# Layer 0's attention issued from a written table, and the second attention's first work drawn into the latent input's last rounds

## The chip, the cores and the metric

The kernel runs on one core of one Trainium2 chip. A core has TensorE (PE: matrix products into PSUM), VectorE (DVE), ScalarE (ACT) and GpSimd (POOL) for elementwise work, and SyncE (SP), which issues most transfers. Each engine works through its own queue in order and waits on semaphores for the others. The metric is the device time in microseconds, from the first to the last instruction with a little around it; lower is better. The program is launched once and computes two whole transformer layers.

## The reference, cut to what matters

```python
for i in range(2):
    h = rms_norm(x, attn_norm_g[i])
    x = x + (diff_attention(h, ...) if i == 0 else mla_attention(h, ...))
    h = rms_norm(x, ffn_norm_g[i])
    x = x + conv_ffn(h, ffn_w_up[i], ffn_conv_w[i], ffn_conv_b[i], ffn_w_down[i])
return rms_norm(x, final_norm_g)

def diff_attention(h, ...):            # 1024 tokens, 8 heads, each with two 64-wide parts c
    q, k, v = jnp.split(h @ w_qkv, 3, axis=-1)
    q, k = rotary on the first 16 of each 64, v is 128 wide
    lam = jnp.exp(jnp.sum(lq1 * lk1)) - jnp.exp(jnp.sum(lq2 * lk2)) + lambda_init
    def block(qb, blk):                # 128 queries at a time, keys up to their 64-token chunk
        p = masked_softmax(jnp.einsum('bqhcd,bkhcd->bhcqk', qb, k) * 64 ** -0.5, mask)
        return jnp.einsum('bhqk,bkhe->bqhe', p[:, :, 0] - lam * p[:, :, 1], v)
    return (rms_norm(o, subln_g) * (1.0 - lambda_init)).reshape(b, s, D_MODEL) @ w_o

def mla_attention(h, ...):             # 16 heads, from latents of rank 384 (q) and 256 (kv)
    proj = h @ w_in
    c_q, c_kv = rms_norm(proj[..., :384]), rms_norm(proj[..., 384:640])
    k_pe = apply_rope(proj[..., 640:])
    q = c_q @ w_uq; k_nope, v = c_kv @ w_ukv
    softmax((q_nope k_nope + q_pe k_pe) * 96 ** -0.5) @ v, then @ w_o
```

All of it is float32; the kernel gets near that with products of split operands.

## The kernel before

**Products.** Every float32 operand is split into a high part (a cast, `hi`, on ScalarE, L127) and a low part (the difference, `lo`, on VectorE or GpSimd, L130), and `mm3` makes one product of three matmuls (L119 to L121). Tiles in SBUF lie in named places of three sizes, `s`, `u` and `h`; PSUM holds two score tiles of two banks (`S`), three single banks (`b`) and one bank `u`, in which the projections gather. These letters are the tile names in the profile.

**Layer 0's attention** (`diff_attention`, `steps`, `DaStep`). The work is 32 steps, t = 4h + p: head h, quarter p, which takes the 256 queries of the row tiles 2p and 2p + 1 (j = 0, 1). A step computes scores for both parts c (L1622, L1623; the j-th row of quarter p has (2p + j + 1) x 128 keys), their maximum on VectorE (L1627, L1631), the exponential on ScalarE (L1637), the reciprocal of the sums (L1647), the product of one with -lambda (L1648), the scaling of part 0 (L147 or L149), and the mix of both parts on VectorE (L1650). One step later the mixed probabilities are transposed (L252), split, and multiplied with v; the quarters 1 and 3 end with a norm over 512 queries (`finish`), one step later still. `rsqrt` in it takes Identity, Ln, Exp and Square on ScalarE (L174 to L177) and two operations on VectorE.

Between these lie the projections of q, k and v, half a sequence at a time: units of 24 matmuls in bank `u` (`da_unit`). `da_complete` frees the bank by a copy on ScalarE for v (L556) or by a shuffle and a product on VectorE for q and k (L237, L238), and goes on with the rotary part (GpSimd, L239 and L240) and the splits. A unit gives its PSUM bank up to the next one only when that is done.

**Order.** `steps` writes the pieces in a plain sequence: scores 0, half a unit, transposes of the step before, weigh 0, scores 1, the rest of the units, the product of the step before, weigh 1, the norm. That sequence is only a priority: a scheduler then sets the order on each engine. Some parts of the kernel are marked `manual_schedule`, and there the engines named take the order as written; the attention steps are not among them.

**The seam to the second attention** (`mla_input`, `mla_heads`). Eight rounds compute the latents of one row tile each (S), followed by transposes into `cq` and `ckv`, and two rounds behind, `values` computes v, copies it to a buffer (ScalarE, L1407) and stores it to `v_d`. The buffers of these copies and of the fetched weights (`self.raw`) are two places used in turn, u14 and u15. In round 7 `heads.first()` projects the first keys and queries; the 64 steps of the second attention are written after round 9, through the same `steps`.

Of the kernel before, what the change touches and what calls it, by code (L numbers as in the profile page):

```python
# [13 lines left out]
ALU = mybir.AluOpType  # L14
# [42 lines left out]
class Trunk:  # L57
# [155 lines left out]
    def load_constants(self):  # L213
# [6 lines left out]
        nc.vector.tensor_scalar_mul(self.g_sub, self.g_sub, 1.0 - LAMBDA_INIT)  # L220
# [60 lines left out]
    def steps(self, attend, units, prepare, n):  # L281
# [3 lines left out]
        for t in range(n + 2):  # L285
# [10 lines left out]
            self.run(u, 1)  # L296
            if before:
                before.turn()
            if now:
                now.weigh(0)  # L300
                now.scores(1)
# [5 lines left out]
            if t >= 2:  # L307
                steps[t - 2].finish()


    def diff_attention(self, o_d, prefetch):
# [24 lines left out]
        def split_w(h, which):  # L336
            if h < DA_HEADS:
                raw = raws.pop((h, which))
                w = self.w([P, 2, D], F32R)
                self.hi(w[:, 0, :], raw)  # L340
                self.lo(w[:, 1, :], raw, w[:, 0, :], nc.gpsimd)
                heads[h]["w", which] = w[:, 0, :], w[:, 1, :]

        def unit(h, which, half):
            hd = heads[h]
            return self.da_unit(R, H, hd["w", which], which, half, hd, tab)
# [168 lines left out]
        def prepare(t):  # L515
            h, p = divmod(t, 4)
            if p == 0:
                split_w(h + 1, 1)
                fetch_w(h + 1, 0)
            if p == 1:  # L520
                split_w(h + 1, 0)
                fetch_w(h + 1, 2)
            if p == 2:
                split_w(h + 1, 2)
            if p == 3:
                fetch_w(h + 2, 1)
            if h + 1 == DA_HEADS:
                prefetch()

# [7 lines left out]
        self.steps(lambda t: DaStep(self, R, *divmod(t, 4), heads, o_d), units, prepare, 4 * DA_HEADS)  # L537

    def da_unit(self, R, H, W, which, half, hd, tab):
# [9 lines left out]
        yield from self.da_complete(R, acc, which, half, hd, tab)  # L549

# [783 lines left out]
    def mla_input(self, W, hts, turns, v_d, heads_of):  # L1334
# [89 lines left out]
        for i in range(NT + 2):  # L1424
            if readies:
                readies.pop(0)()
            if i == NT - 1:
                heads.share(1, 0)
                heads.first()
# [19 lines left out]
            if i == NT:  # L1449
                rotary(1)  # L1450
                heads.share(1, 1)
        return heads

    def mla_heads(self, cT, v_d, o_d):
# [5 lines left out]
        v_ring, q_ring, t_ring = self.ring("s13", "s4"), self.ring("s1", "s10", "s5", "s9"), self.ring("h10", "h11", "h8")  # L1460
        k_places, kT = ["s0", "s11", "s12", "s8"], []
# [3 lines left out]
            P=self.ring("u6", "u7", "u8", "u9", "u12"), pT=self.ring("u0", "u1", "u10", "u11"), o=self.ring("h4", "h5", "h6", "h7"),  # L1465
# [59 lines left out]
        def first():  # L1525
# [496 lines left out]
```

## Time and profile before

| | |
|---|---|
| median of 3 runs | 2427.79 us (2427.32 to 2431.45) |
| the profiled execution | 2430.68 us, its span 2428.9 us |
| TensorE busy | 2355.0 us (97%) |
| VectorE, ScalarE, GpSimd busy | 1916.0, 1305.3, 618.5 us |
| granted TensorE clock, mean | 0.996 |
| layer 0's attention, heads 0 to 6 | 53 to 459 us of the span |
| the seam between latent input and second attention | 1329 to 1366 us |

Matmuls overlap and their ends are modelled, so a busy TensorE is not one that starts a matmul as often as it could. A row of the waits gives who waited for whom, the time in total, how often, and the longest. A row of a timeline gives start, duration, engine, line, operation, tiles written and read, and in brackets the idle time before it and what ended it.

### The profile page before, as it was taken

To read this page: it belongs to the slowest core of one execution; us is meant where nothing else is said; L and a number is where in the kernel's file an instruction comes from. 1 tells how busy PE (TensorE), PEld (TensorE's weight loads), DVE (VectorE), ACT (ScalarE), POOL (GpSimd) and SP (SyncE) were. 2 spreads that over 40 slices of the span, in tenths; PEclk is the share of its full clock that TensorE was granted. 3 is DMA by queue.
4 is the path that set the end of the run, shared out by engine and by line. 5 is a ranking of instruction groups with operands and counts; after the bars stand their busy time and mean duration, and the time that the engine had idled before them with its cause. 6 is when DMAs were issued, how large, how long until landed. Compare 5 with 4: busy or idle time off the path is not lost.

```text
span 2428.9 us, 32660 instructions
## 1 busy us (share of the span) xinstructions
PE 2355.0 (97%) x11936; PEld 1997.5 (82%) x11936; DVE 1916.0 (79%) x3111; ACT 1305.3 (54%) x2446; POOL 618.5 (25%) x489
## 2 busy tenths in 40 slices
PE   7999999999999999999999999999999999999998
PEld 6888787887888888878899788988878888887886
DVE  6667776857888888889964777887488888888997
ACT  5677777755444444444445777776244444444444
POOL 4545454424100000000041666665330000000001
PEclk9999999999999999999999999999999999999999
DMA  4111111223322222554221211114322222227502
GB/s 161 40 35 44 35 35 44 100 93 100 99 82 79 87 78 88 187 175 131 72 103 46 77 40 29 49 59 134 96 87 87 79 87 87 78 86 278 172 3 78
DMA packets 95792, 213.91 MB, mean 88 GB/s; under 512 B 8720, under 2 KB 33936, under 8 KB 95632
## 3 DMA queue, kind: packets, MB, share of 16 engines
q1 hardware_dynamic: 86448, 184.04, 23.1%
q10 hardware_dynamic: 9184, 27.79, 3.1%
q8 instruction: 94, 1.54, 0.3%
q14 instruction: 66, 0.54, 0.1%
HBM read 159.37 MB, written 52.43 MB: 87 GB/s over the span
## 4 chain that ended last, share of the span: by engine, by line
PE 82%; DVE 7%; ACT 5%; DMA 3%; issue 2%; POOL 1%; SPq 0%; DVEq 0%; POOLq 0%; ACTq 0%
PE S L119 13%; PE S L121 13%; PE S L120 13%; PE b L119 8%; PE b L120 8%; PE b L121 8%; PE u L119 4%; PE u L120 4%; PE u L121 4%; PE b L252 3%; DMA u<-g_d 2%; PE u L1727 1%; DVE s L130 1%; PE u L1726 1%; ACT s L127 1%
## 5 line engine op out<-in xcount | busy, mean ns | idle before, releaser
L167 POOL TENSOR_TENSOR st<-st,mhalf 128x1 f32<-128x1 f32 x56 | 36.6, 654 | 1314.1 <-DVE st L164 1305.5
L127 ACT CAST u<-h 128x512 fp32r<-128x512 f32 (+2 forms) x242 | 145.9, 619 | 297.4 <-DVE h L847 277.7
L119 PE MATMUL S<-s,u 128*128 128x512 f32 (+1 forms) x768 | 290.5, 378 | 7.6 <-ACT s L127 2.6
L121 PE MATMUL S<-s,u 128*128 128x512 f32 (+1 forms) x768 | 289.5, 377 | 0.1
L120 PE MATMUL S<-s,u 128*128 128x512 f32 (+1 forms) x768 | 289.4, 377 | 0.0
L119 PE MATMUL b<-s,u 128*128 128x512 f32 x588 | 231.0, 393 | 1.5 <-DVE u L130 0.8
L121 PE MATMUL b<-s,u 128*128 128x512 f32 x588 | 229.3, 390 | 0.0
L120 PE MATMUL b<-s,u 128*128 128x512 f32 x588 | 229.2, 390 | 0.0
L904 DVE SCALAR_TENSOR_TENSOR u<-u,conv,u 128x1023 f32<-128x1023 f32 (+1 forms) x176 | 225.8, 1283 | 1.4 <-ACT u L900 1.4
L149 POOL TENSOR_TENSOR u<-u,st 128x384 f32<-128x384 f32 (+7 forms) x160 | 169.7, 1068 | 151.0 <-DVE st L1712 106.7
L127 ACT CAST s<-u 128x512 fp32r<-128x512 f32 (+2 forms) x230 | 145.0, 666 | 108.2 <-PE u L121 35.8
L119 PE MATMUL u<-s,s 128*128 128x512 f32 (+1 forms) x440 | 178.5, 406 | 13.4 <-ACT h L556 7.0
L130 DVE TENSOR_TENSOR u<-b,u 128x512 fp32r<-128x512 f32 (+1 forms) x256 | 157.4, 629 | 29.4 <-ACT u L127 28.0
L119 PEld LDWEIGHTS S<-s,u 128*128 128x128 f32 x768 | 145.2, 189 | 35.1 <-ACT s L127 5.5
L121 PE MATMUL u<-s,s 128*128 128x512 f32 (+1 forms) x440 | 173.2, 394 | 0.0
L120 PE MATMUL u<-s,s 128*128 128x512 f32 (+1 forms) x440 | 172.8, 393 | 0.0
L121 PEld LDWEIGHTS S<-s,u 128*128 128x128 f32 x768 | 145.2, 189 | 26.6 <-DVE u L130 0.5
L120 PEld LDWEIGHTS S<-s,u 128*128 128x128 f32 x768 | 145.3, 189 | 26.1
L130 DVE TENSOR_TENSOR s<-u,s 128x512 fp32r<-128x512 f32 (+2 forms) x210 | 150.0, 746 | 12.4 <-ACT s L127 12.2
L127 ACT CAST u<-b 128x512 fp32r<-128x512 f32 (+1 forms) x256 | 133.2, 550 | 37.9 <-PE b L252 28.9
L907 ACT ACTIVATE u<-u 128x1024 f32<-128x1024 f32 x44 | 46.7, 1062 | 187.5 <-DVE u L904 187.5
L130 DVE TENSOR_TENSOR u<-h,u 128x512 fp32r<-128x512 f32 x164 | 112.7, 687 | 32.5 <-ACT u L127 31.5
(270 smaller groups left out, 6561.1 us busy)
## 6 DMA issues: line engine op xcount, KB each, us to landing
u<-in_ffn_up SPq DMA_DIRECT2D x88, 512.0 KB, 3.9
g_d<-u ACTq DMA_DIRECT2D x44, 512.0 KB, 2.6
u<-in_ffn_down SPq DMA_DIRECT2D x66, 256.0 KB, 4.8
u<-g_d SPq DMA_DIRECT2D x62, 256.0 KB, 4.4
s<-in_da_wqkv SPq DMA_DIRECT2D x23, 512.0 KB, 3.6
x_d<-u SPq DMA_DIRECT2D x16, 512.0 KB, 2.9
s<-x_d SPq DMA_DIRECT2D x8, 1024.0 KB, 10.8
u<-o_d SPq DMA_DIRECT2D x24, 256.0 KB, 2.9
```

The costliest lines, as they stand in the source:

```text
L119: mm(out, lh, rl, start=first, stop=False, skip_group_check=onto)
L120: mm(out, lh, rh, start=False, stop=False, skip_group_check=onto)
L121: mm(out, ll, rh, start=False, stop=last, skip_group_check=onto)
L127: self.nc.scalar.copy(out, src)
L130: (eng or self.nc.vector).tensor_sub(out, src, hi.bitcast(F32))
L149: self.nc.gpsimd.tensor_mul(x, x, s.to_broadcast(list(x.shape)))
L167: nc.gpsimd.tensor_tensor(r, s, self.mhalf, ALU.pow)
L252: self.nc.tensor.transpose(ps[:, j * P : (j + 1) * P], probs[t][:, k : k + P], self.ident)
L904: nc.vector.scalar_tensor_tensor(t[half][:, back:], u[half][:, : S - back], w, t[half][:, back:], ALU.mult, ALU.add)
L907: nc.scalar.activation(t[0], t[0], AF.Silu)
L1726: nc.tensor.matmul(o[:, c0:], v, al, start=kb == 0, stop=False)
L1727: nc.tensor.matmul(o[:, c0:], v, ah, start=False, stop=kb == 2 * p + 1)
```

## The change

It has two parts, and a smaller one inside the first.

1. Layer 0's attention goes through `da_steps`. Steps 0 to 27 (heads 0 to 6) are cut into pieces of one or two instructions, and a table, `DA_SCORE`, with one line for each quarter (a slot), writes the order of the pieces of up to five steps. All four compute engines are under `manual_schedule` there, so each takes its pieces in this order. In the table a name is a piece of the step of that slot, with ' for each step earlier, and + for the next step. S, M, E, I, C, X are scores, maximum, exponential, reciprocal, scaling and mix (with j, and a or b for part c); T, H, L, A are transposes, high part, low part and product of a group of 256 keys; O copies the result; Q, F, R, N are the norm's squares, sum, root and the rest; Wh and Wl split weights; U and V are the units, with 0 and 1 for their halves of 12 matmuls. Head 7's steps are written in a plain sequence again and left to the scheduler.
2. The product with -lambda moves to VectorE, and the norm loses its Identity: Ln reads the PSUM sum itself, and the first VectorE operation reads it too. The sign of `g_sub` turns with it.
3. `steps` becomes a generator. The first key and first query unit are written in round 6, the second query in round 7, and the first two steps of the second attention in the rounds 8 and 9 of the latent input. Some places change (`q_ring`, `k_places`, the ring `P`). As the fetch of the next pair's weights is now written between the last two `values`, it takes one turn of the two buffers.

```diff
+    DA_SCORE = (
+        "S0 S1 M0 Up O'' R2''' V0 X1' R3''' N1''' M1 T1' Ua E0a H1' L1' Uka E1a T0' H0' T2' Ukb Ukc V1 E0b L0' I0 E1b A0' N2''' T3'",
...
+    def da_steps(self, attend, units, prepare, n):
+        E = mybir.EngineType
+        region = ExitStack()
+        region.enter_context(self.tc.manual_schedule(engines={E.PE, E.DVE, E.Activation, E.Pool}))
+        steps, last = [], 28
+        for t in range(-1, n + 2):
...
+            if t == last:
+                region.close()
...
+            for name in self.DA_SCORE[t % 4].split():
+                step = t - name.count("'") + name.count("+")
+                if 0 <= step < min(n, last):
+                    steps[step](name.strip("+'"))
+            if t < last:
+                continue
...
-        self.steps(lambda t: DaStep(self, R, *divmod(t, 4), heads, o_d), units, prepare, 4 * DA_HEADS)
+        self.da_steps(lambda t: DaStep(self, R, *divmod(t, 4), heads, o_d), units, prepare, 4 * DA_HEADS)
...
-        nc.vector.reciprocal(l, l)
-        nc.scalar.mul(w, l[:, 1:2], k.neglam)
+    def invert(self, j):
+        k = self.k
+        l = self.l[j]
+        k.nc.vector.reciprocal(l, l)
+        k.nc.vector.tensor_scalar_mul(l[:, 1:2], l[:, 1:2], k.neglam)
...
+    def root(self, x):
+        k, act = self.k, self.k.nc.scalar.activation
+        if x == 0:
+            self.r, self.tmp = self.R.fin([P, 512]), self.R.fin([P, 512])
+            act(self.tmp, self.ss, AF.Ln, bias=k.eps, scale=1.0 / P)
+        elif x == 1:
+            act(self.r, self.tmp, AF.Exp, scale=-0.5)
+        else:
+            act(self.tmp, self.r, AF.Square, scale=(0.5 / P) ** 0.5)
+    def newton(self, x):
+        k, stt = self.k, self.k.nc.vector.scalar_tensor_tensor
+        if x == 0:
+            stt(self.tmp, self.ss, EPS * P, self.tmp, ALU.add, ALU.mult)
...
+            if i == NT - 2:
+                heads.share(1, 0)
+                heads.first(0, 2)
             if i == NT - 1:
-                heads.share(1, 0)
-                heads.first()
+                heads.first(4)
...
+            if i >= 8:
+                heads.early()
...
-        v_ring, q_ring, t_ring = self.ring("s13", "s4"), self.ring("s1", "s10", "s5", "s9"), self.ring("h10", "h11", "h8")
-        k_places, kT = ["s0", "s11", "s12", "s8"], []
+        v_ring, q_ring, t_ring = self.ring("s13", "s4"), self.ring("s1", "s11", "s5", "s9"), self.ring("h10", "h11", "h8")
+        k_places, kT = ["s0", "s10", "s12", "s8"], []
...
+        work = [self.steps(attend, units, prepare, 4 * MLA_HEADS)]
+        def early():
+            self.run(work, 1)
```

What this makes of the queues, at three places. First TensorE's queue in a steady head where the scores of quarter 0 end and those of quarter 1 begin (S is a score tile, `h` and the second `u` the query parts). Before:

```order
L1622 MATMUL S_1707<-u_269_1337,h_55_147 128x256 [waits Activation_49]
L1623 MATMUL S_1707<-u_269_1337,u_298_1464 128x256
L1622 MATMUL S_1707<-u_269_1337,h_56_148 128x256
L1623 MATMUL S_1707<-u_269_1337,u_298_1464 128x256
L252 MATMUL b_1677<-ident,u_308_1513 128x128 [waits Activation_49]
L252 MATMUL b_1685<-ident,u_308_1513 128x128 [waits Activation_49]
L1622 MATMUL S_1818<-u_269_1337,h_55_147 128x384 [waits DVE_49,Activation_49]
```

And now, where the last products and transposes of the quarter before end:

```order
L121 MATMUL b_1727<-u_332_1701,u_204_1038 128x256
L1851 MATMUL b_1735<-ident,u_303_1570 128x128 [waits PE_49]
L1851 MATMUL b_1735<-ident,u_311_1619 128x128 x2
L1804 MATMUL S_1739<-u_275_1421,h_55_147 128x384 [waits Activation_49]
L1805 MATMUL S_1739<-u_275_1421,u_285_1478 128x384
L1804 MATMUL S_1739<-u_275_1421,h_56_148 128x384
```

The scores of 256 keys stood two transposes ahead of those of 384; now a whole unit, four groups of transposes and a product lie between the two.

Second, ScalarE's queue around the copy that frees bank `u` behind a unit of v (L556 before, L636 now). Before:

```order
L1665 COPY h_270_1342<-b_1343 128x256 [waits PE_49]
L174 ACTIVATE h_275_1360<-b_1356,eps 128x512 [waits PE_49]
L127 CAST u_286_1411<-b_1406 128x512 [waits PE_49]
L175 ACTIVATE h_276_1361<-h_275_1360 128x512 [waits Activation_49]
L556 COPY h_324_1590<-u_1517 128x512 [waits PE_49]
```

And now, in slot 0 to 1 of a head:

```order
L1830 ACTIVATE u_330_1694,st_329_1693<-S_1648,st_323_1676 128x256 [waits DVE_49]
L127 CAST u_332_1701<-b_1696 128x512 [waits PE_49]
L668 ACTIVATE u_328_1691<-h_317_1635 64x512
L1830 ACTIVATE u_326_1686,st_325_1685<-S_1643,st_320_1653 128x128
L1830 ACTIVATE u_330_1694,st_329_1693<-S_1648,st_323_1676 128x256
L636 COPY h_337_1746<-u_1660 128x512 [waits PE_49]
```

The steps of the norm that stood ahead of the copy are elsewhere; two exponentials stand there.

Third, SyncE's queue at the seam, with the stores of v and the fetch of the second pair's weights (`in_mla_w`). Before:

```order
L1408 DMA v_d<-u_2013_11819 128x8x128 [waits DMAHW1_49,Activation_49]
L1408 DMA v_d<-u_2018_11854 128x8x128 [waits DMAHW2_49,Activation_49]
L135 DMA u_2027_11906<-in_mla_w 128x1024 [waits DMAHW3_49,DMAHW4_49,DMAHW2_49,DMAHW0_49]
L1408 DMA v_d<-u_2024_11886 128x8x128 [waits Activation_49]
L135 DMA u_2057_12026<-v_d 128x1024 [waits DMAHW5_49,DMAHW7_49,DMAHW4_49,DMAHW1_49]
```

And now:

```order
L1549 DMA v_d<-u_1919_11613 128x8x128 [waits DMAHW0_49,Activation_49]
L1549 DMA v_d<-u_1933_11726 128x8x128 [waits DMAHW1_49,Activation_49]
L135 DMA u_1944_11793<-in_mla_w 128x1024 [waits DMAHW3_49,DMAHW7_49,DMAHW2_49,DMAHW1_49]
L1549 DMA v_d<-u_1938_11761 128x8x128 [waits Activation_49]
L1549 DMA v_d<-u_1957_11857 128x8x128 [waits DMAHW4_49,Activation_49]
```

The fetch has moved one store ahead, and the last two stores follow it.

More of the change, by code (lines that the diff above doesn't have):

```diff
@@ L279, in run, with steps @@
                 n -= 1
-    def steps(self, attend, units, prepare, n):
+    def steps(self, attend, units, prepare, n, apart=False):
         steps = []
@@ L1523, in mla_heads, with first @@
         split_w(0)
-        def first():
-            self.run([u() for u in pair_units(0)[::2]])
+        def first(*which):
+            self.run([pair_units(0)[x]() for x in which])
         def own(i, y):
```

318 lines of the change are left out of this document (239 added, 79 removed), and 3 rows, old and new, of the table DA_SCORE.

## The prediction

> **What bounds the kernel now.** I read the page first, then the stages, then the waits of TensorE in the stage that the table rewrites, then single waits there, and last the seam between the latent input and the second attention. The page's busy time:
>
> ```profile
> PE 2355.0 (97%) x11936; PEld 1997.5 (82%) x11936; DVE 1916.0 (79%) x3111; ACT 1305.3 (54%) x2446; POOL 618.5 (25%) x489
> ```
>
> TensorE is the bound; the change removes none of its matmuls, so it can only win time in which TensorE waits. The stages (busy time of each engine; the first is heads 0 to 6 of layer 0, the second head 7 and the start of the output projection, the third the seam):
>
> ```profile
> core 0: us, PE busy (x) PEld busy (x) DVE busy (x) ACT busy (x) POOL busy (x), PEclk, DMA share, GB/s
> 53.00:459.00 406.00, 388.26 (x2066) 329.35 (x2066) 292.22 (x509) 291.29 (x611) 207.94 (x148) 0.99 0.13 44
> 459.00:545.00 86.00, 84.21 (x445) 71.41 (x445) 56.92 (x87) 52.10 (x108) 27.82 (x22) 1.00 0.30 99
> 1329.00:1366.00 37.00, 31.67 (x152) 24.30 (x151) 26.08 (x59) 28.14 (x61) 20.94 (x15) 0.95 0.37 118
> ```
>
> Heads 0 to 6 take 406 us, 58 a head, and TensorE is without work for 406 - 388.3 = 17.7 of them, although VectorE and ScalarE are each busy only 72% (292/406, 291/406). So no engine is full: the order makes the waits. What ended them, in 53 to 459:
>
> ```profile
> PE u L119 <- ACT h L556: 7.0, 6, 1.3
> PE S L1622 <- ACT u L1637: 6.6, 5, 1.5
> PE u L119 <- DVE h L238: 3.2, 4, 1.4
> PE b L186 <- DVE u L130: 0.9, 3, 0.3
> ```
>
> That is again 17.7, in 18 waits. 10.2 of it is for the one PSUM bank u of the projections, freed late by ScalarE's copy (L556) or VectorE's rotary product (L238); 6.6 is for an exponential (L1637) that frees a score bank. The listed wait is too small, as TensorE's timeline behind one of them shows (start, duration):
>
> ```profile
> 450.30 0.79 PE L119 MATMUL u<-s,s 128*128 128x512 f32 x1 [1.44 <-DVE h L238]
> 450.89 0.63 PE L120 MATMUL u<-s,s 128*128 128x512 f32 x1
> 451.32 0.63 PE L121 MATMUL u<-s,s 128*128 128x512 f32 x1
> ...
> 456.28 0.39 PE L121 MATMUL u<-s,s 128*128 128x512 f32 x1
> 456.50 0.39 PE L119 MATMUL u<-s,s 128*128 128x512 f32 x1
> ```
>
> A matmul of 512 columns is listed 0.39 long, yet the next starts 0.22 later (456.28, 456.50). A wait that begins at a matmul's listed end hides 0.39 - 0.22 = 0.17, so 18 waits hide 3.1. And behind this wait the matmuls start 0.43 apart (450.89, 451.32) until about 456.0: 5.1 us at half rate, some 13 matmuls at 0.2 each, 2.6 us lost. **Removable in heads 0 to 6: 17.7 + 3.1 + 2.6 = 23.4 us.**
>
> The Trainium skill (TensorE: Matmul & The Clock Gate, "Why this matters for your kernels") wants pauses kept under about 3 us. The pause above is 1.44 and the half rate came all the same, so the trace does not bear out that threshold; by the rule the 2.6 would not hang on this wait and would stay, and the sum below would end 2.6 higher.
>
> **The table, part by part.** Why a copy is late: TensorE's wait at 261 and ScalarE's timeline before it.
>
> ```profile
> 259.38 0.49 PE L252 MATMUL b<-ident,u 128*128 128x128 f32 x3
> 261.20 0.50 PE L119 MATMUL u<-s,s 128*128 128x512 f32 x1 [1.33 <-ACT h L556]
> ```
>
> ```profile
> 258.60 0.36 ACT L1665 COPY h<-b 128x256 f32<-128x256 f32 x1
> 258.98 0.69 ACT L174 ACTIVATE h<-b,eps 128x512 f32<-128x512 f32 x1
> 259.57 0.58 ACT L127 CAST u<-b 128x512 fp32r<-128x512 f32 x1
> 260.03 0.64 ACT L175 ACTIVATE h<-h 128x512 f32<-128x512 f32 x1
> 260.56 0.58 ACT L556 COPY h<-u 128x512 f32<-128x512 f32 x1
> ```
>
> The bank's last matmul was issued before the three transposes at 259.38; the copy started 1.2 after these, behind two steps of a norm (L174, L175) that nobody waited for. The table puts this copy directly behind two exponentials in slot 1 and, in slot 3, behind two squares but ahead of the three casts H, so L556 and L1637 should go as releasers. What is late next I read from the table by sums of durations, from two stretches of the second of these heads, ScalarE's and VectorE's timeline (start, duration):
>
> ```profile
> 280.13 1.11 ACT L1637 ACTIVATE u<-S,st 128x1024 f32<-128x1024 f32 x1 [0.62 <-DVE st L1627]
> 281.14 0.19 ACT L1637 ACTIVATION_READ_ACCUMULATOR u<-S,st 128x1 f32 x1
> 281.23 0.36 ACT L1665 COPY h<-b 128x256 f32<-128x256 f32 x1
> 281.50 0.69 ACT L174 ACTIVATE h<-b,eps 128x512 f32<-128x512 f32 x1
> 282.08 0.28 ACT L1648 ACTIVATE st<-st,neglam 128x1 f32<-128x1 f32 x1
> 282.27 1.14 ACT L147 ACTIVATE u<-u,st 128x1024 f32<-128x1024 f32 x1
> ```
>
> ```profile
> 271.48 0.73 DVE L237 STREAM_SHUFFLE h<-u 128x512 f32<-128x512 f32 x1
> 272.11 0.67 DVE L238 TENSOR_TENSOR h<-u,s 128x512 f32<-128x512 f32 x1
> ...
> 278.81 1.22 DVE L1627 TENSOR_REDUCE st<-S 128x1 f32<-128x1024 f32 x1
> 280.06 1.40 DVE L571 SCALAR_TENSOR_TENSOR u<-h,u 64x512 fp32r<-64x512 f32 x2
> 281.50 0.17 DVE L1647 RECIPROCAL st<-st 128x2 f32<-128x2 f32 x1
> ```
>
> *The long chain*, from S1 of quarter 3 to its transposes T1 in the next slot: two peaks 2.4, the second exponential 1.11 + 0.19, reciprocal and its product 0.3, scale 1.14, mix 1.28 (below): 6.4, and with six hand-offs of some 0.07, an estimate, 6.8. In TensorE's row stand between them U1, A1, F, A2, the two S of the next head and V0: 24 + 2 matmuls of 512 columns at 0.23 (6.0), and by columns, as an estimate, nine products of 256 and three of 128 (1.2) and 1536 columns of scores (0.7): 7.9. It fits by 1.1.
>
> *Bank u* changes hands six times a head. Freeing it by shuffle and product takes 0.73 + 0.67 = 1.4, by copy 0.6. TensorE's work in between, by the same spacing and at 0.11 to 0.16 a transpose (three in 0.49 at 259.38): 1.7 (U1 to V0, slot 1), 1.9 (V1 to U0, slot 2), 1.9 (U1 to U0, slot 2), 1.2 against the copy (slot 3), 2.4 (slot 3 to 0), 1.4 against the copy (slot 0 to 1). Each fits if VectorE or ScalarE comes to it within 0.3 to 1.0. Half of the six missing by 0.3 is 0.9 a head, **6.3 in seven heads, my value for what stays**; the ends are 0.2 a head (1.4) and 1.8 a head (12.6), the last being every hand-off late by 0.3.
>
> *Work removed and added.* ScalarE loses eight 0.28 products with neglam (L1648) and two L174 a head: 2.2 + 1.4 = 3.6 of its 291/7 = 41.6. VectorE gains eight 128x1 products, 1.4 by the 0.17 of L1647, on 292/7 = 41.7. At a head of (406 - 23.4 + 6.3)/7 = 55.6 that is 68% and 78%, so neither becomes the bound by its sum; this costs nothing as long as the queue order holds. The norm's sum now stays in its PSUM bank until N1, which the table sets just ahead of that bank's next transposes: 0 to 0.3 a head, inside the ends. Products, transposes and scores keep count and size. The first slots up to 53 keep their order, and in head 7 the free scheduler fills with the same projections: nothing, +-2.
>
> **The seam.** SyncE's fetch of the second pair's weights moves ahead of the last two stores of v, and the first key and query projections move from the last latent round into the one before. What TensorE and ScalarE waited for in 1329 to 1366:
>
> ```profile
> PE u L1726 <- DVE h L1730: 2.3, 1, 2.3
> ```
>
> ```profile
> ACT u L127 <- DMA u<-in_mla_w: 1.3, 1, 1.3
> ```
>
> TensorE lacks work for 37 - 31.7 = 5.3 there. The scores still stand behind the same transposes, so steps 0 and 1 hardly move; what moves are fifteen projection matmuls and the fetch. The 1.3 on in_mla_w goes, as the fetch needs the buffer of an earlier store. Between the two products of which the second waited 2.3 now stand six more score matmuls of 512 columns, 1.4. I take **4.0**: that 1.4, the 1.3, and 1.3 for the half rate there (clock 0.95 of 37 is 1.9). Ends: 8 (all of 5.3, the clock and the hidden parts) and -2: the last v copies now reuse the buffer of the store just ahead instead of the one before, and ScalarE would sit behind that store, with bank u and the first product behind it. On SyncE the store of v tile 6 is queued behind the moved fetch, which waits only for the store before.
>
> **The sum.** The profiled execution took 2430.7 (span 2428.9), 2.9 above the median 2427.8. From it: -23.4 + 6.3 - 4.0 = -21.1, 2409.6; on the median **2406.7**. Ends of the costs: 23.4 - 1.4 + 8 = 30 gives 2398; 23.4 - 12.6 - 2 = 9 gives 2419.
>
> **Rivals.** *Port, slower.* VectorE's mix of 1024 twice, and GpSimd's weight split beside the first:
>
> ```profile
> 226.42 3.41 DVE L1650 SCALAR_TENSOR_TENSOR u<-u,st,u 128x1024 f32<-128x1024 f32 x1
> ...
> 283.99 1.28 DVE L1650 SCALAR_TENSOR_TENSOR u<-u,st,u 128x1024 f32<-128x1024 f32 x1
> ```
>
> ```profile
> 226.29 2.46 POOL L130 TENSOR_TENSOR s<-s,s 128x1024 fp32r<-128x1024 f32 x1 [5.08 <-ACT s L127]
> ```
>
> A mix that starts while GpSimd runs ends 2.13 later, and now everything behind it on VectorE is held in a fixed order. If three mixes a head (X1 of quarters 3, 1 and 2, beside the rotary adds and the q parts) meet it in full, less the 1.1 of slack in quarter 3 and half that, my estimate, in the others: 1.0 + 1.6 + 1.6 = 4.2, plus 0.9, is 5.1 a head or 36, against 23.4 removed: 2427.8 + 12 = 2440 if the seam gives nothing. It decides from 3.4 a head on. For it: 30 us of GpSimd a head (208/7) in 55.6. Against: GpSimd's busiest slot is 1, where the mixes are the small ones. 13%.
> The Trainium skill (SBUF — State Buffer, "SBUF: two separate sides") calls this port pair an exclusive lock for VectorE operations with two SBUF inputs against GpSimd; 3.41 against 1.28 agrees.
>
> *Waits that come back.* 2.2 to 3.2 a head stay since each queue is now in order and a late cast holds the copy behind it: 23.4 - 19 is 4, 2423 without the seam, 2419 with it. 15%. *The whole of it*, nothing stays and the seam closes: 2398 or less, 8%. *The table does nothing that counts*, its waits equal to the scheduler's, and the seam gives as little: 2428, 3%. Forecast 61%, 2412 to 2400.
>
> The bound for telling from no change is 0.2%, 4.9 us, so faster means under 2422.9. Forecast, the waits that come back and the whole of it: 84%; same 3%; slower 13%. The range 2398 to 2423 leaves out the port rival, part of the equal case and about 4% below.
>
> **What would show it.** Right: heads 0 to 6 take near 389 in place of 406, TensorE's releasers L556 and L1637 vanish from that stretch, the half rate at 450 is gone, and ScalarE no longer waits for in_mla_w. Wrong: T1 of quarter 3 or the first matmul of U or V waiting in every head for VectorE, with mixes over 2 us beside GpSimd; or a new wait of the v copies for a store at the seam.

## The result, and the profile after

| | before | changed |
|---|---|---|
| median of 12 runs | 2430.28 us (2426.72 to 2432.03) | 2427.67 us (2424.48 to 2431.32) |
| ratio, 95% interval | | 0.9991 (0.9983 to 0.9998) |
| the profiled execution, its span | 2430.68, 2428.9 | 2427.72, 2425.9 |

The forecast was 21 us less, 2406.7, in a range of 2398 to 2423. The change brought 2 to 3. The page of the changed kernel, and the three stages that the prediction used:

```profile
PE 2355.7 (97%) x11936; PEld 1999.6 (82%) x11936; DVE 1960.6 (81%) x3175; ACT 1290.5 (53%) x2366; POOL 623.5 (26%) x489
```

```profile
core 0: us, PE busy (x) PEld busy (x) DVE busy (x) ACT busy (x) POOL busy (x), PEclk, DMA share, GB/s
53.00:459.00 406.00, 393.91 (x2105) 335.67 (x2103) 342.01 (x577) 285.86 (x560) 222.22 (x153) 0.99 0.14 48
459.00:545.00 86.00, 78.90 (x403) 65.95 (x402) 51.74 (x83) 41.63 (x78) 21.67 (x19) 0.96 0.30 94
1329.00:1366.00 37.00, 32.26 (x154) 25.34 (x153) 26.09 (x59) 27.69 (x59) 21.33 (x15) 0.91 0.39 118
```

TensorE is busier by 5.7 in the first stretch (393.9 against 388.3), and less busy by 5.3 in the second (78.9 against 84.2). What was won in heads 0 to 6 is missing right behind them. The waits of TensorE say the same. First the steady part, 53 to 425 us (who waited for whom, total, times, longest):

```profile
PE b L1896 <- POOL h L130: 2.6, 6, 0.5
PE u L119 <- DVE h L657: 2.0, 1, 2.0
PE b L119 <- DVE u L130: 1.9, 6, 0.3
```

The copy (L556, now L636) and the exponential (L1637, now L1830) are gone from the list, as forecast, and 6.5 of waits are left in place of the 14.7 that before had up to 425 (the 17.7 of the prediction reach to 459). Then 425 to 560 us:

```profile
PE S L119 <- ACT h L127: 5.9, 1, 5.9
PE b L1851 <- DVE u L1843: 5.3, 2, 3.9
PE S L121 <- POOL s L130: 1.0, 1, 1.0
PE u L119 <- DVE h L657: 0.3, 1, 0.3
```

Two new waits, 3.9 where the table ends and 5.9 in the output projection, are together larger than all that is listed up to 425.

To follow a gain through queues of different order I count TensorE's work: each matmul at its undisturbed spacing in the trace (0.227 us for 512 columns, 0.175, 0.132, 0.119 and 0.061 for 384, 288, 256 and 128, 0.109 for a transpose), 2298 us in every kernel. Below stands how far each kernel is ahead of before when it has done the same work (negative: behind). The kernels besides "after" are those of the experiments.

```
work us | before at | after  table  seam   hold   vec    vec_sum7  ops    ops_seam  neg   before
        |           |        _only  _only  _split _split           _only  _vec      _only _vec
 100    |   125     |  -0.1    0.3    0.3    0.7   -0.8     0.1    -1.1    0.0       0.1   0.1   head 0 done
 380    |   431     |  11.1   11.5    0.5   11.9   10.4    11.3     4.7    5.8       5.0   0.2   steady heads done
 400    |   457     |  10.7   11.9    0.5   17.1   15.0    16.0    10.6   11.7       7.7   4.6   head 7 begins
 480    |   542     |   9.4   10.9    0.3    0.6   16.3    12.1    11.2   12.3       9.6   4.4
 500    |   562     |   1.6    2.8    0.3    0.6    8.0    11.6     8.6    3.3       7.3   4.4   output projection
1220    |  1297     |   1.9    2.6   -0.4    1.8    8.8    13.7     9.3    4.4       2.3   2.7   before the seam
1320    |  1411     |   0.4    2.4   -0.4    2.7    7.9    12.5    10.1    5.3       3.0   2.2   behind the seam
1400    |  1498     |   4.1    1.8    3.3    2.0   11.7    16.3     9.0    9.1       2.4   2.2
1700    |  1818     |   3.1   -6.6    4.0   -6.3   11.3    16.9     2.9    9.7      -4.3   2.4   second attention done
2290    |  2412     |   3.0   -8.0    1.5   -9.5   10.4    14.1     1.7    9.2      -3.6   2.2   end
```

These are single executions; they lie within 2.6 us of their kernels' medians. Where the text says that a kernel is ahead at a time, it is the time of before. The column "after" tells where the forecast went: nothing in head 0, 11 in the heads behind it, 8 given back between 542 and 562, 1.5 lost at the seam, 3.7 won behind it.

**Where the table ends.** VectorE's mix of 768 in the last slot of the table, the same mix one head earlier, and GpSimd at that time (start, duration):

```profile
367.46 1.47 DVE L1843 SCALAR_TENSOR_TENSOR u<-u,st,u 128x768 f32<-128x768 f32 x1 [0.50 <-ACT u L147]
...
424.24 5.41 DVE L1843 SCALAR_TENSOR_TENSOR u<-u,st,u 128x768 f32<-128x768 f32 x1 [1.45 <-ACT u L147]
```

```profile
422.43 2.88 POOL L130 TENSOR_TENSOR h<-h,u 64x512 fp32r<-64x512 f32 x2 [2.45 <-issue]
425.28 2.34 POOL L130 TENSOR_TENSOR s<-s,s 128x1024 fp32r<-128x1024 f32 x1
427.59 1.25 POOL L130 TENSOR_TENSOR h<-h,h 128x512 fp32r<-128x512 f32 x1
```

The `s<-s,s` of 425.28 is a weight split of the output projection, written two steps later in the program. The table holds the order of its own pieces only; the scheduler set this one between two of them. GpSimd then worked from 422.43 to 428.84 without a pause, and the mix ended 0.8 behind it. TensorE stood before the transposes of that mix, and started the next matmuls at half rate:

```profile
429.71 2.40 PE L1851 MATMUL b<-ident,u 128*128 128x128 f32 x10 [3.93 <-DVE u L1843]
431.76 0.78 PE L119 MATMUL u<-s,s 128*128 128x512 f32 x1
432.33 0.63 PE L120 MATMUL u<-s,s 128*128 128x512 f32 x1
```

The Trainium skill (SBUF — State Buffer, "SBUF: two separate sides") has it that whoever of the two starts first holds the port pair for its whole instruction. That the mix takes longer beside GpSimd agrees; that it stayed behind three GpSimd rows in turn, 4.6 us from its listed start to 428.84, is more than the page says, with the reserve that spans on GpSimd are rough.

**The output projection.** GpSimd's last input of the last norm's sum, in before and then in the changed kernel; that sum on TensorE, SyncE's store of the result, and TensorE's next row tile, all three in the changed kernel:

```profile
523.51 1.35 POOL L130 TENSOR_TENSOR h<-h,h 128x512 fp32r<-128x512 f32 x1 [0.89 <-ACT h L1669]
```

```profile
523.68 1.30 POOL L130 TENSOR_TENSOR h<-h,h 128x512 fp32r<-128x512 f32 x1 [7.48 <-ACT h L1888]
```

```profile
528.46 0.40 PE L1896 MATMUL b<-h,ones 128*128 128x512 f32 x1
```

```profile
533.53 0.33 SPq L1917 DMA_DIRECT2D o_d<-h  x1
```

```profile
533.72 0.39 PE L121 MATMUL S<-s,h 128*128 128x512 f32 x1
540.00 0.80 PE L119 MATMUL S<-s,h 128*128 128x512 f32 x1 [5.89 <-ACT h L127]
540.59 0.63 PE L120 MATMUL S<-s,h 128*128 128x512 f32 x1
```

From the sum to the first product that needs it (norm, store, load, split) the chain takes 540.0 - 528.5 = 11.5. TensorE hides it behind what it has left. The first half of the output projection has 96 products in score banks (`S<-s,s`), 21.8 us of work that may be done at any time. In before, 58 of them stood in TensorE's queue ahead of the sum and 38 behind it: 8.6, and 5.4 of the next row tile, cover the chain. In the changed kernel all 96 stand ahead, and 5.4 is all that is left. So the sum ran at 528.46, as late as in before (528.8), although its input was there at 524.98 and TensorE was 9.4 us ahead; then it waited 5.9 and ran at half rate. The lead had been spent on work that was cover. And the chain itself had won nothing: in before the sum's last input was ready at 523.51 + 1.35 = 524.86, in the changed kernel at 524.98.

### The profile page after: what moved, and what is told of

The parts are those of the page before. It is cut to its first block, busy times and chain, and to the rows that moved or that the text cites. A ratio compares the mean times of both kernels' runs of the same rounds, so it can differ in the third digit from the quotient of the medians.

```text
span 2425.9 us, 32597 instructions
## 1 busy us (share of the span) xinstructions
PE 2355.7 (97%) x11936; PEld 1999.6 (82%) x11936; DVE 1960.6 (81%) x3175; ACT 1290.5 (53%) x2366; POOL 623.5 (26%) x489
## 4 chain that ended last, share of the span: by engine, by line
PE 82%; DVE 7%; DMA 4%; ACT 3%; POOL 2%; issue 2%; SPq 0%; POOLq 0%; DVEq 0%; ACTq 0%
PE S L119 13%; PE S L121 13%; PE S L120 13%; PE b L119 8%; PE b L120 8%; PE b L121 8%; PE u L119 3%; PE u L121 3%; PE u L120 3%; PE b L252 2%; DVE s L130 2%; PE u L1961 1%; PE u L1960 1%; PE S L1804 1%; PE S L1805 1%
## 5 line engine op out<-in xcount | busy, mean ns | idle before, releaser
L127 ACT CAST s<-u 128x512 fp32r<-128x512 f32 (+3 forms) x230 | 144.9, 665 | 112.3 <-PE u L121 35.5
```

Source lines behind the costliest of these rows:

```text
L127: self.nc.scalar.copy(out, src)
```

## The experiments

The runs were made on four chips. Each ratio, with its 95% interval, is to runs of before on the same chip (medians of before there: 2430.2 to 2431.4); where two rows of different chips are compared, the ratios and their intervals are the safer guide.

| kernel | median us | ratio to before |
|---|---|---|
| table_only | 2436.9 | 1.0034 (1.0021 to 1.0046) |
| seam_only | 2428.3 | 0.9992 (0.9984 to 1.0001) |
| sum_first7 | 2424.0 | 0.9978 (0.9969 to 0.9986) |
| hold_split | 2439.0 | 1.0038 (1.0024 to 1.0052) |
| vec_split | 2419.4 | 0.9953 (0.9940 to 0.9965) |
| vec_split_sum7 | 2415.0 | 0.9934 (0.9922 to 0.9947) |
| vec_split_last30 | 2425.6 | 0.9980 (0.9971 to 0.9989) |
| table_only_sum7 | 2426.3 | 0.9984 (0.9975 to 0.9993) |
| ops_only | 2430.9 | 1.0007 (0.9997 to 1.0016) |
| head0_vec | 2426.9 | 0.9987 (0.9978 to 0.9995) |
| head0_vec_27 | 2416.6 | 0.9944 (0.9931 to 0.9956) |
| proj_late | 2415.6 | 0.9942 (0.9929 to 0.9956) |
| ops_seam_vec | 2421.9 | 0.9968 (0.9956 to 0.9981) |
| neg_only | 2431.8 | 1.0002 (0.9994 to 1.0011) |
| before_vec | 2428.4 | 0.9987 (0.9978 to 0.9996) |

### The two parts alone

`table_only` is the changed kernel with the seam of before; `seam_only` is before with the new seam (its `steps` yields, and is run from round 8 on).

```diff
 table_only, against the changed kernel
-            if i == NT - 2: heads.share(1, 0); heads.first(0, 2)
-            if i == NT - 1: heads.first(4)
+            if i == NT - 1: heads.share(1, 0); heads.first(0, 2, 4)
-            if i >= 8: heads.early()
 and q_ring, k_places, P as in before
```

> The table for layer 0's attention alone, the seam as in the kernel before. At equal work TensorE's lead over before was 11.1 us at the end of head 6, 1.6 behind the output projection and 2.9 at the end, of which 2.2 came between 1295 and 1494 us, where the seam lies. If the two parts add up, this kernel has the same 11 and the same loss at the output projection, and lacks the 2.2: 2430 us, no gain on before. Rival: the 2.2 is not the seam's own but an echo of the lead; then 2427.5.

> The seam alone (projections and first steps of the second attention written two rounds sooner), layer 0's attention as in the kernel before. If the parts add up: 2.2 below before, 2428 us, with TensorE no faster in 1329 to 1410 (there the changed kernel lost 1.5) and the gain behind it, in the second attention's first heads. Rival: the gain needs the earlier start that the table gives; then 2430. My prediction had 4.0 at the seam itself: 2426.

Measured: 2436.9 and 2428.3. Alone the seam gives the 2 expected, which its interval does not tell from nothing; alone the table is 6.6 slower than before, though up to 1411 us it stands as well as the changed kernel (2.4 ahead). The 9 are lost in the second attention, whose text is the same. There TensorE's queue repeats itself every two heads, in one of two ways. As a fingerprint, the numbers of TensorE instructions from one group of products with values to the next:

```
cycle A: 43 5 30 13 22 23 41 12 31 26 26        (after, seam_only; before in its last heads)
cycle B: 29 23 15 29 12 31 29 20 35 16 8 25     (table_only, from the start)
```

TensorE's timeline at the same place of two neighbouring turns, in the changed kernel and then in `table_only`:

```profile
1472.44 0.52 PE L252 MATMUL b<-ident,u 128*128 128x128 f32 x3
...
1513.97 0.52 PE L252 MATMUL b<-ident,u 128*128 128x128 f32 x3
```

```profile
1494.20 0.55 PE L252 MATMUL b<-ident,u 128*128 128x128 f32 x3 [0.84 <-DVE u L130]
...
1537.94 0.55 PE L252 MATMUL b<-ident,u 128*128 128x128 f32 x3 [0.85 <-DVE u L130]
```

41.5 us against 43.7 for two heads. Both cycles come with either seam (`hold_split` and `head0_vec` below have the new seam and cycle B), and the five kernels in cycle B all lost 7 to 9 between 1411 and 1818 us, while the others won up to 4.6 or lost at most 1.6. Which of them the scheduler falls into hangs on edits far ahead: `table_only_sum7`, below, differs from `table_only` only in layer 0, and leaves cycle B. From here on the queue says before a run which cycle a kernel will have, and the expectations use it.

### Two cures that were tried first

`sum_first7` puts 24 of the 96 products (row 7) behind the sum; `hold_split` puts the splits of the output projection's weights behind the GpSimd work written before them. `issue_after` sets an order in one engine's queue and adds no wait.

```diff
 sum_first7
+                        if i == 7:
+                            held.enter_context(self.tc.issue_after(self.last_sum))
 hold_split
+                pool = [i for i in nc.cur_bb.bb.instructions if i.engine == mybir.EngineType.Pool][-1]
+                with self.tc.issue_after(pool):
                     prefetch()
```

> The changed kernel, with the last row tile's 24 products of the output projection's first half (row 7 of 8) queued behind the last norm's sum (L1896) on TensorE; nothing else is written differently. Theory (the fill is spent): the changed kernel runs all 96 such products before that sum, so that behind it only 24 products (5.4 us) cover a chain of 11.3 us; with 24 more behind it the 6.05 wait at 534 to 540 and the half rate after it (2.3) go: 8 less than the changed kernel, 2420. Rival (head 7 is a chain of its own): the products held back leave TensorE idle before the sum instead, and the time stays at 2426 to 2428.

Measured 2424.0, 3.6 less than the changed kernel, not 8. (Its profiled execution took 2428.1, 4 above the median: a 512 KB store took 5.6 us there, against 2.9.) In its trace the wait of 5.9 is gone, and TensorE waits 2.0 ahead of the sum instead, for its input, and 3.1 behind it for the next link of the chain, the normalized first row tile. The sum ran at 525.17, 3.3 sooner, which is about what the median won: the products held back can free no more than that, as the input comes no sooner. So a part of the loss is cover and the rest is the chain, as the rival said. How the 8 divide is known from the medians alone; in this execution TensorE stood at 562 us no better than in the changed kernel (0.8 ahead against 1.6).

> The changed kernel, with GpSimd's splits of the output projection's weights queued behind the GpSimd work written before them; in the changed kernel the scheduler puts the first one at 425 us, beside VectorE's mix of 768, which takes 5.41 instead of 1.47. Theory (lock at the table's end, and fill spent): the mix takes under 2.5, TensorE's wait of 4.09 at 426 to 430 and the half rate after it (1.3) go, and the order that follows from it leaves 72 of the 96 products behind the last sum, so the wait of 6.05 goes too: 2427.7 - 5.4 - 8.3 = 2414. Rival (only the place of the products counts): 2419 to 2420, as the time won at 430 is waited for again in head 7. Rival (head 7 is a chain of its own): 2426 to 2428.

Measured 2439.0, against every theory. At 457 us it was 17.1 ahead (the changed kernel 10.7): without the split at 425 the wait at the table's end is gone. Then it met the same lock in head 7. VectorE's and GpSimd's timelines, and TensorE's:

```profile
452.63 3.16 DVE L1845 SCALAR_TENSOR_TENSOR u<-u,st 128x128 f32<-128x128 f32 x2 [0.65 <-POOL u L149]
```

```profile
453.13 2.39 POOL L130 TENSOR_TENSOR s<-s,s 128x1024 fp32r<-128x1024 f32 x1
```

```profile
457.31 0.55 PE L119 MATMUL b<-u,u 128*128 128x256 f32 x1 [4.53 <-DVE u L130]
```

A mix of 128 and the next one of 256 (the row bears the first one's shape) took 3.16 beside the split that had been moved. The low parts behind it, for which TensorE waited 4.5, came late, and 6.5 of the lead were gone; by 478 us nearly all of it was, behind a wait of 3.3 for GpSimd's low part ahead of a norm's sum and more half rate. How much of the 4.5 is the lock alone is not shown. The 72 products that now stood behind the sum were of no use any more, and the second attention fell into cycle B (6.3 behind at its end). So the next kernels take the split off GpSimd.

### The split on VectorE

```diff
-                    W.append(k.split(places[len(W)], raws.pop(0), nc.vector if len(W) % 2 else None))
+                    W.append(k.split(places[len(W)], raws.pop(0), nc.vector))
```

> The changed kernel, with all splits of the output projections' weights (low parts, 128x1024) on VectorE; every other one was on GpSimd. Theory (lock at the table's end): the mix of 768 at 424 us takes about 1.5 instead of 5.41, TensorE's wait of 4.1 there and the half rate after it (1.3) go, VectorE gets 1.2 for each of two splits. The 96 products of the output projection still stand ahead of the last sum, so the 6.05 wait there stays, only sooner: 2427.7 - 5.4 = 2422.3. Rival (head 7 is a chain of its own, an earlier start is waited off in it): 2427. The second attention is scheduled as in the changed kernel.

> The same with the output projection's last 24 products of the first half queued behind the last sum as well. If the two losses are separate they add up: 5.4 and the 3.6 that those products gave alone (2424.0 against 2427.7): 2418.5. If both are the same time, lost once: 2422 to 2424.

> Splits on VectorE and the table used for two more steps (steps 28 and 29, the first half of head 7, too). By the order 72 of the 96 products then stand behind the last sum. Theory (the lead of heads 0 to 6 is kept where no lock waits at the table's end and enough products stand behind the last sum): TensorE's lead over before is 11 or more at 420 us and still 9 to 12 behind the output projection at 600, with the second attention's 3.7: 2417. Rival (head 7 as a chain eats the lead wherever the table ends): 2424 to 2427.

> The table alone (seam as before), with the same 24 products behind the last sum. By the order the second attention now runs as in the kernel before (its last heads in the cycle of 41.5 us per two heads), where the table alone had the other cycle of 43.7 in all heads. Theory (which cycle the scheduler falls into decides, not the seam): 2436.9 - 3.6 for the products - 8 for the cycle = 2425. Rival (the second attention's 8 us hang on something else of the table): 2433.

Measured: 2419.4, 2415.0, 2425.6, 2426.3. The one line takes 8.2 from the changed kernel (5.4 expected), and the mix at the table's end is shorter; TensorE still waits 1.3 for it:

```profile
425.66 2.04 DVE L1843 SCALAR_TENSOR_TENSOR u<-u,st,u 128x768 f32<-128x768 f32 x1
```

`vec_split` is 15.0 ahead at 457 and 16.3 at 542, and loses 8.3 to the output projection, as the changed kernel lost 7.8: with no product behind the sum that price hardly depends on the lead. (Its chain is earlier, though: the last input of the sum is there at 519.1.) With 24 products behind it (`vec_split_sum7`) that loss is 0.5, while ahead of the sum the lead falls from 17.5 at 522 us to 12.1; 11.6 are left at 562. That version beats both kernels, before by 16 and the changed one by 13. It took 4.5 off `vec_split`, where 3.6 were expected.

`vec_split_last30` had 72 products behind the sum, and failed for another reason. Steps 28 and 29 now lay inside the table's part, where VectorE's queue keeps the written order, and the splits written there stood ahead of the mix:

```profile
439.03 2.36 DVE L130 TENSOR_TENSOR s<-s,s 128x1024 fp32r<-128x1024 f32 x2 [1.70 <-ACT s L127]
...
441.95 1.27 DVE L1843 SCALAR_TENSOR_TENSOR u<-u,st,u 128x1024 f32<-128x1024 f32 x1
```

TensorE waited 5.3 for that mix, until 443.28. `table_only_sum7`, whose queue showed the second attention of before, came out 10.6 under `table_only` (2425 expected). By the traces some 3 of that are won by 562 us, and 7.4 between 1411 and 1818, where `table_only` loses 9.0 and this kernel 1.6: the cycle decides, not the seam's text.

### What the arithmetic did

> The kernel before, with the change's arithmetic alone: the product with -lambda on VectorE, the norm without its Identity, no table and the old seam. My prediction gave this nothing by itself. By the order the second attention falls into the cycle of 43.7 us per two heads from the start. Theory (a change far upstream flips the cycle): level with before until 1330 us (within 2), then 8 to 9 lost between 1400 and 1820: 2439. Rival (the cycle belongs to table or seam): 2430.

> As vec_split_sum7, and in head 0 also the weight split of 60.8 us on VectorE instead of GpSimd. There two mixes of 256 and one of 384 ran beside GpSimd's splits (3.73 for the two, 2.73), then bank u came free late: 2.12 of waiting and 1.7 of half rate at 65 us. Lock theory: the two mixes of 256 take about 1.0, bank u comes free 1 to 2 sooner, and TensorE's lead at 120 us grows by 2 to 3.8. Rival (head 0 is held by its own start): lead unchanged. By the order the second attention falls into the slow cycle: 2415.0 - 3 + 8.5 = 2420.5 by the theory, 2423.5 by the rival.

> The same with the table ended one step sooner (step 27 left to the scheduler); by the order the second attention then has the fast cycle. If head 0's 3 are won and the end of the table costs no more than before: 2415.0 - 3 = 2412. Rival (the place where the table ends sets new waits): 2415 to 2420.

> As vec_split_sum7, but the first key and query projections of the second attention are written in round 7 as in the kernel before; its first two steps stay in rounds 8 and 9. My prediction put 4.0 at the seam down to these projections and the fetch. Theory (the seam's own moves gain nothing, its gain comes from the cycle of the second attention, which this kernel has too): 2415 within 1.5, no change. Rival (the projections matter): 2417 to 2419.

```diff
 ops_only, against before (the norm reads its PSUM sum as in the change)
-        nc.scalar.mul(w, l[:, 1:2], k.neglam)
+        nc.vector.tensor_scalar_mul(w, w, k.neglam)
 head0_vec, against vec_split_sum7
-                self.lo(st.w[:, 1, :], st.raw, st.w[:, 0, :], nc.gpsimd)
+                self.lo(..., nc.vector if (h, which) == (1, 0) else nc.gpsimd)
 head0_vec_27: head0_vec with last = 27
 proj_late: vec_split_sum7 with heads.first(0, 2, 4) in round 7
```

`ops_only` took 2430.9, level with before, but neither theory had it: it was 9.3 ahead at the seam and lost 7 in the second attention, in cycle B. That it ended at the rival's 2430 is luck. The edit to which I had given nothing put TensorE 4.7 ahead at 431 us, where the whole change has 11.1; at 457 the two are level (10.6 and 10.7), and behind the output projection the arithmetic alone is far ahead (8.6 against 1.6). Its waits from 53 to 425 us, 9.6 in all, which were 7.0 for the copy, 5.1 for the exponential and 1.7 for the rotary product, 14.7 in all, in before:

```profile
PE u L119 <- DVE h L237: 4.6, 6, 0.8
PE u L119 <- ACT h L555: 2.8, 6, 0.6
PE S L1621 <- ACT u L1636: 1.8, 2, 1.0
```

Head 0: a row of two mixes, 256 and 384 (it bears the first one's shape, and the expectation counted it wrongly as two of 256), beside a split, TensorE behind them, and the same mixes in `head0_vec`, in the timelines of the two kernels:

```profile
60.05 3.73 DVE L1843 SCALAR_TENSOR_TENSOR u<-u,st 128x256 f32<-128x256 f32 x2
```

```profile
60.81 2.56 POOL L130 TENSOR_TENSOR s<-s,s 128x1024 fp32r<-128x1024 f32 x1
```

```profile
65.06 0.50 PE L119 MATMUL u<-s,s 128*128 128x512 f32 x1 [1.96 <-DVE h L657]
```

```profile
60.35 1.61 DVE L1846 SCALAR_TENSOR_TENSOR u<-u,st 128x256 f32<-128x256 f32 x2
```

The mixes took 1.6 in place of 3.7, and the lead at 125 us was 1.7 larger than in `vec_split_sum7` (2 to 3.8 expected): the lock in head 0 is real, and worth some 1 to 3. (The executions of the nine kernels with the table and this head unchanged lie between -0.9 and 0.8 there, `head0_vec` at 1.8 and `head0_vec_27` at 2.1.) In time it did not show: `head0_vec` took 2426.9, outside theory and rival, as cycle B cost it 13.4 against `vec_split_sum7` between 1411 and 1818 (8.5 expected), and `head0_vec_27`, in cycle A, ended at 2416.6, with new waits where its table ends. `proj_late` equals `vec_split_sum7` (2415.6 and 2415.0): the projections drawn into round 6 give nothing that shows.

Three more told what belongs to the table (`ops_seam_vec` is `vec_split` without it) and to the edit of the split (`before_vec`).

> No table: the kernel before with the change's arithmetic, its seam, and the output projections' splits on VectorE. By the order the second attention has the fast cycle, as in vec_split (2419.4), from which only the table is missing. Theory (the table itself is worth what the steady heads show): they take 55.9 with the table and 56.6 with the arithmetic alone, 0.7 in each of six heads, so 2423.5. Rival (the arithmetic gives all that lasts): 2419 or less.

> The kernel before with one edit: the product with -lambda on VectorE. The arithmetic as a whole gave TensorE a lead of 4.7 at 430 us and 8.6 at 552. Theory (ScalarE's eight small products a head, which stand ahead of copy and exponentials, held TensorE): half or more of it, a lead of 2.5 to 4.7 at 430. Rival (the norm's Identity and its PSUM read did it): 0 to 1. By the order the second attention falls into the slow cycle, which takes 6 to 7 back: 2432 by the theory, 2436 by the rival.

> Control: the kernel before with the output projections' splits all on VectorE and nothing else; the second attention's order stays as it was. Theory (the 8 us that this edit gave the changed kernel belong to the lock at the table's end): before has no long mix there (1.82 against 1.0 for the one of 768), so 2430 within 2.5. Rival (GpSimd's splits cost as much without the table): 2424 or less.

Measured: 2421.9, 2431.8, 2428.4. Without the table 2.4 are missing (4 expected), and the intervals of `vec_split` and `ops_seam_vec` overlap, so that this is not clear of noise: at 431 us the table's lead over the arithmetic alone is 4.6, at the end 1.2. The product with -lambda alone gives 5.0 at 431 us, all that the arithmetic gives there, and the slow cycle takes it back as expected. That its time came out at the 2432 of the theory is in part luck: its lead grew to 9.6 at 542, and 3.6 of it went at one place between 1031 and 1056 us, with a wait of 3.5 and half rate in this execution. The control came within its range, but not for the reason given: `before_vec` is 4.4 to 4.6 ahead from 457 to 562, so GpSimd's splits cost the kernel before as well. Of the 8.2 of `vec_split`, some 2 to 4 belong to that.

## Why the prediction was wrong, point by point

Of the 21.1 that the sum forecast, the profiled executions have 3.0. Heads 0 to 6 gave 10.7 in place of 17.1; head 7 and the output projection lost 9.1 in place of nothing; the seam lost 1.5 in place of winning 4.0; and 3.7 came behind it by luck of the schedule. Small pieces make up the rest.

- **The waits to be removed, and 6.3 that stay: right in the steady heads, not in the stage.** Steady heads take 55.8 (head 4's first score starts at 269.5, head 5's at 325.3), against 55.6 forecast. But they had taken 57.7 in before, not the 58 of the mean, so each won 1.9 and not 2.4; head 0 won nothing, and 3.9 and half rate were lost where the table ends. Heads 0 to 6 thus take some 395 by the equal-work count, not the 389 named as the sign. Of listed waits 6.5 are left in 53 to 425. They are not those forecast: six times 0.4 for GpSimd's low part ahead of the norm's sum, six times 0.3 for VectorE's low part, and bank u only in head 0.
- **"This costs nothing as long as the queue order holds" (the arithmetic): it cost nothing, but it gained, and for that I had no term.** I weighed the moved products by ScalarE's busy time, 68% of a head. They stood in its queue ahead of what TensorE waits for, and moving those with -lambda alone gave 5.0 by 431 us. So of the 11.1 won by then, 5.0 were to be had without the table. No run here has the table with the old arithmetic, so what the table gives without it is open.
- **"In head 7 the free scheduler fills with the same projections: nothing, +-2": this is the step that failed.** It lost 1.3 up to 542 us, and 7.8 behind that. I had asked what head 7 does with the same work, not what a scheduler does with time won ahead of it: it brought the output projection's products forward, which had been the cover of the last norm. Nor did head 7's chain of elementwise work come sooner: the last sum's input was ready at 524.98, in before at 524.86. Holding part of the products back returned 3.6 by itself and 4.5 on top of `vec_split`. The other runs agree, and the table is not needed for it: where no product stands behind the sum, 7.8 to 9.0 are lost between 542 and 562 us (`after`, `table_only`, `vec_split`, and `ops_seam_vec`, which has no table); with 22 of them behind it `ops_only` and `neg_only` lose 2.6 and 2.3, and `before_vec`, with the 38 of before, loses nothing.
- **The port rival: right as a mechanism, wrong in its place.** It was to decide on three mixes in every head. In the steady heads the same two mixes of 256 and 384 meet the split too, and no wait of TensorE for VectorE follows there (the pair took 1.6 in head 0 without the split):

```profile
340.38 3.77 DVE L1843 SCALAR_TENSOR_TENSOR u<-u,st 128x256 f32<-128x256 f32 x2
```

  It decided where there was no slack: 1 to 3 in head 0, and some 5 where the table ends (3.9 and the half rate after it).
- **The seam, 4.0: wrong.** The wait for L1730 went; in its place TensorE waits for the first exponentials of the early steps. ScalarE's wait on in_mla_w, which was to go, is still there and has grown from 1.3 to 2.2. TensorE's waits in 1329 to 1366, and this one of ScalarE:

```profile
PE S L119 <- ACT u L1940: 3.7, 4, 1.4
PE b L1523 <- DVE S L1938: 0.5, 1, 0.5
```

```profile
ACT u L127 <- DMA u<-in_mla_w: 2.2, 1, 2.2
```

  TensorE's time without work fell by 0.6 there (5.3 to 4.7), and the granted clock from 0.95 to 0.91. Over the seam the changed kernel lost 1.5; of the other kernels in the table with the new seam none won more than 0.9 there. Behind it, it won 3.7, because the second attention came into cycle A two turns, four heads, sooner. I had no term for that.
- **The half rate at 450 is gone**, and came back at 432, at 541 and at 65. The Trainium skill (TensorE: Matmul & The Clock Gate, "Why this matters for your kernels") wants gaps under about 3 us. Behind gaps of 3.93 and 5.89 it agrees, behind 1.96 at 65 it does not; a gap of 1.39 at 451.7 was followed by none. The length of a gap does not decide alone: `proj_late` has the same gap at the same place, and its matmuls go on 0.23 apart. And the 1.44 at 450 in before, which the prediction took by itself, stood only four matmuls behind a gap of 1.46. The rows of `proj_late`, and that of before:

```profile
65.69 0.50 PE L119 MATMUL u<-s,s 128*128 128x512 f32 x1 [1.96 <-DVE h L657]
...
66.50 0.40 PE L119 MATMUL u<-s,s 128*128 128x512 f32 x1
66.73 0.39 PE L120 MATMUL u<-s,s 128*128 128x512 f32 x1
```

```profile
447.67 0.50 PE L1622 MATMUL S<-u,h 128*128 128x512 f32 x1 [1.46 <-ACT u L1637]
```

What stays open: why the cycle B costs 1.1 more a head. The waits listed for VectorE's low part in it (2.1 in 1500 to 1590, none in the changed kernel) make about half of that, and no run here forced one cycle or the other with all else equal. Open too is why head 7's chain in the changed kernel came no sooner than in before, and whether the table leaves anything to the end.

## What to carry to other kernels

Time won on the bounding engine is worth only what the next fixed chain leaves of it: look for the last chain of the stage, count what stands behind its first link, and keep that cover there, before pricing waits ahead of it. A written order holds only what is written in it; work of a later stage that the scheduler may float between its pieces has to be kept out or written down, and a moved conflict is not a removed one (`hold_split`). Where a scheduler sets the rest of the program, compare its queues far behind the edit too: here an edit of eight small products turned an attention 1000 us later into a cycle that was 7 to 9 us slower, more than most of the effects that were looked for.

## What was not expected of the hardware

A VectorE mix did not come in between GpSimd instructions that follow one another: at 424.24 it took 5.41 in place of 1.47, ending 0.8 behind the last of three GpSimd rows, and a pair of 256 and 384 took 3.73 in place of 1.61. And TensorE's half rate came after a gap of 1.96 in the changed kernel and not after the same gap of 1.96 in `proj_late`; in before it came with two gaps of 1.46 and 1.44 close together.
